# Two transformer blocks on one core: keeping the split weight blocks that two token streams share

## The chip, the cores and the metric

The kernel runs on one core of a Trainium2 chip. The metric is device time in microseconds (us) of one execution, as the median of several runs. Everything is float32 outside and inside; the large products are made in float32r, a form in which the tensor engine takes one pass per product, and float32's accuracy is kept by splitting each operand into a high and a low part and adding three products (high by high, high by low, low by high).

## The reference, cut to what matters

Two blocks follow each other on 512 tokens of 2048 channels. The first is a gated convolution beside a differential attention. The second has two recurrences (a gated delta rule of 8 heads and an RWKV-7 scan of 16 heads), and these run over a context of 256 tokens first and then over the 512 latent tokens. Both streams are multiplied by the same weight matrix:

```python
h = rmsnorm(x, norm_g[layer]) * (1.0 + scale[:, None]) + shift[:, None]
hc = rmsnorm(ctx, norm_g[layer]) * (1.0 + scale_c) + shift_c
u = h @ w_in[layer]
uc = hc @ w_in[layer]
ya_c, ya = gdn_mixer(uc[..., :GDN_COLS], u[..., :GDN_COLS], ...)
yb_c, yb = rwkv_mixer(uc[..., GDN_COLS:], u[..., GDN_COLS:], ...)
x = x + gate[:, None] * (jnp.concatenate([ya, yb], axis=-1) @ w_out[layer])
return rmsnorm(x, final_norm_g)
```

The context's own output isn't used; only the states that its recurrences leave go into the latent stream.

## The kernel before, in words

Activations lie with channels on partitions and tokens along the free dimension. The second block's input weights `w2` are 69 blocks of 128 output channels by 2048 input channels. `mblock` (L111) makes one block's product into a PSUM bank (pool `pd`, two banks) in two halves of 8 input tiles; `products` (L120) makes a half. It loads the half, 512 KB, into `wraw` (three buffers) by a DMA on SyncE's queue (L127), splits it (`split`, L103: a cast on ScalarE gives `whi`, L104, and a subtraction on VectorE gives `wlo`, L105), and issues 24 products (L136), three for each input tile. `whi` and `wlo` have two buffers each, so the split of one half waits until the tensor engine is done with the half before the last. While the context's gates, keys and values are made, every second subtraction goes to GpSimd (`K.on_pool = 2`).

The stages in the order of time, with the times of the profile:

- 0 to 456 us: the first block's modulation, gates and some steps of its convolution.
- 456 to 777 us: the context's products, 37 blocks or 74 halves with 256 columns each. These blocks are the gates (`B_GATE`), 8 keys and 8 values of the delta rule, 4 low-rank blocks (`B_LO`), and 8 keys and 8 values of the other recurrence. Their results go to DRAM as `kc` and `rc`. `ctx_gdn`, the delta rule over the context, runs in the gaps, head by head; a head loads `cgk` and `cgv` from `kc`.
- 777 to 2275 us: the rest of the first block with the remaining context recurrences in its gaps.
- 2275 to 3112 us: `mixers_gdn`. The gates and `B_LO` are first multiplied while `h` is made, in quarters of 4 input tiles (`K.pre` in `block1`); then for each of 8 heads the blocks Q, K, V, Z and `gdn_core`. The head's output goes out as `yd`. The last two heads also take the first pairs' inputs of the other recurrence (`mixed`: blocks R, K, V, Z).
- 3112 to 3900 us: `mixers_rwkv`, with the later pairs' `mixed` blocks and the first half of the output's products as filling.
- 3900 to 4056 us: the rest of the output's products and the final norm.

The program is written in Tile, which orders each engine's instructions ahead of time by priority and by its own estimate of when each is ready; matmuls of a burst of `K.burst` are put ahead of others (`FIRST`). Each engine, and SyncE's DMA queue, then works strictly in that order: a DMA whose wait isn't over holds up all behind it.

Of the kernel before, what the change touches and what calls it, by code (L numbers as in the profile page):

```python
# [55 lines left out]
EARLY, HELD = 6, 4     # gates made along with h, gates held back until the convolution's norm  # L56
# [8 lines left out]
def setup(ctx, tc, A):  # L65
# [14 lines left out]
    K.n_split = K.on_pool = 0  # L80
    K.cs, K.pre = {}, {}
# [29 lines left out]
def mblock(K, wap, act, T, k0=0, k1=16, half=8):  # L111
    """psum [128, T] = block^T . act, with act a list of (hi, lo) tiles for k = k0 .. k1."""
    ps = K.pd.tile([128, 512], F32, name="pd")
    for ka in range(k0, k1, half):
        products(K, ps, wap, act[ka - k0:], T, ka, min(half, k1 - ka), k0, k1)
        K.fill()
    return ps[:, :T]


def products(K, ps, wap, act, T, ka, w, k0, k1):  # L120
    """The w products from k = ka on of the block's in ps. K.burst of them follow each other, as the array is slow
    to change over from and to others."""
    nc, tc = K.nc, K.tc
    raw = K.wp.tile([128, 8, 128], F32, name="wraw")
    hi = K.wp.tile([128, 8, 128], F32R, name="whi", bufs=2)
    lo = K.wp.tile([128, 8, 128], F32R, name="wlo", bufs=2)
    nc.sync.dma_start(raw[:, :w], wap[:, ka:ka + w, :])  # L127
    K.n_split += 1
    split(K, hi[:, :w], lo[:, :w], raw[:, :w], nc.gpsimd if K.on_pool and K.n_split % K.on_pool == 0 else nc.vector)
    for k in range(w):  # L130
# [9 lines left out]
def rsqrt(K, pool, src, shape, a, eps, name, eng=None, exact=False):  # L140
    """(src * a + eps) ** -0.5, src may be in PSUM: a guess from the bits, then Newton's steps."""
# [21 lines left out]
def exp_acc(K, pool, x, shape, name):  # L163
    """exp to float32's accuracy: 2^n exactly, the rest from exp(r/2)^2 near 0."""
# [17 lines left out]
def silu2(K, pool, dst, src, name):  # L182
    """dst = 2 * silu(src)."""
    th = pool.tile(list(dst.shape), F32, name=name + "_th")
    K.nc.scalar.activation(th, src, AF.Tanh, scale=0.5)
    K.nc.vector.scalar_tensor_tensor(dst, th, 1.0, src, op0=ALU.add, op1=ALU.mult)


def ada_vec(K, pool, key, cols):
    """silu of the conditioning vectors, as the stationary columns of the modulation's products."""  # L190
# [10 lines left out]
def ada_steps(K, key, wname, bias, groups, nj, pe=True, pool=None):  # L201
    """In steps: K.mod[key][:, block, j] = silu(c_j) . w_ada + b_ada, channels on partitions; 512 columns a group.
    Without pe the vector engine sums over the 16 blocks of inputs, for j = 0."""
# [32 lines left out]
def colsum(K, src, T, w="ones", bank="px0"):  # L236
    """psum [128, T] = sum over partitions (of each half for bones), on every partition."""
# [5 lines left out]
def run(it, n=10000):  # L243
    """n more steps of it, if there are so many."""
# [4 lines left out]
class ChanSS:  # L249
    """Sums the squares of n channel tiles over all channels; rinv() gives (a * sum + eps) ** -0.5 on every  # L250
    partition. The tensor engine sums over the tiles, too, or else GpSimd does."""
# [29 lines left out]
def rsqrt_bcast(K, pool, p, row, T, a, eps, name, px, g):  # L281
    """psum [128, T] = (a * x + eps) ** -0.5 with x in psum p, tokens on partitions (g columns for each 128 of
    them); for g = 2 the columns go to a half of the partitions each. row [128, T] is overwritten."""
# [15 lines left out]
def load_rms(K, pool, src, T, name):  # L299
    """rsqrt(mean of squares over the channels + EPS) of a [16, 128, T] array in DRAM, on every partition."""  # L300
# [8 lines left out]
def modulate(*a):  # L309
    """hi/lo of xt * rinv * g * (1 + scale) + shift, xt = get(k), hi and lo in the tiles that put() returns."""  # L310
    return list(modulate_steps(*a))
# [24 lines left out]
# ------------------------------------------------------------------ unit lower triangular inverses  # L336
def inv64(K, pool, upool, nm, n, d, px, tmp):
    """nm [128, n, 64] holds -M^T of two 64 x 64 units a tile (halves of the partitions), M strictly
    lower in time order; tmp [128, n, 64] is overwritten. Returns U = ((I + M)^-1)^T alike, and T of the 32-blocks."""
# [38 lines left out]
    # 32 -> 64; e: the earlier 32-block of the unit, l: the later  # L378
# [29 lines left out]
# ------------------------------------------------------------------ gated delta rule  # L408
def gdn_gates(K, pool, kpool, ps, T, s):
    """ps [128, T]: rows 0-7 g d0, 32-39 g d1, 64-71 beta d0, 96-103 beta d1."""  # L410
# [23 lines left out]
    # cumulative sums over each 64 tokens: inside each 16, then of the 16s' totals  # L434
# [58 lines left out]
def cumsum(K, g):  # L493
    """In place over the last axis (64): pairs are summed first, then the sums' cumulative sums give the rest."""
# [13 lines left out]
def gdn_prep(K, pool, ps, T, ti, name, nb=2):  # L508
    """Centred convolution and silu of one channel tile, for q and k then unit columns a token; v is
    left doubled."""  # L510
# [26 lines left out]
def gdn_core(K, pool, cpool, h, q, k, v, T, s, gates, S):  # L537
    """One head of one stream. Returns the sum of both directions' outputs (channels on partitions) for
    the latent stream, else None; S[d] holds the states and is updated."""
# [5 lines left out]
    # row broadcasts of the cumulative gates, both directions at a time  # L545
# [26 lines left out]
    def gram(b, nm, mask):  # L572
        """b . k in compact form: [128, nt, 64] of each 64-chunk with itself, and with the tile's other."""
# [24 lines left out]
    for d in range(2):  # L598
# [31 lines left out]
        # dd: -M^T of the chunks; dx: -M^T from the first chunk to the second  # L630
        u64, u32, t32, ys = inv64(K, pool, pool, dd, nt, d, px[d], pool.tile([128, nt, 64], F32, name="iv_tmp"))
        # T of the first chunk: its 32-blocks and T_l Y between
# [29 lines left out]
        # the tail keys  # L662
# [1095 lines left out]
```

## Time and profile before

| what | value |
|---|---|
| time, median of 3 runs | 4048.28 us (4042.07 to 4054.17) |
| span of the profiled execution (it is none of the three; its own time isn't listed apart) | 4056.2 us |
| busy PE / DVE / ACT / POOL | 94% / 69% / 34% / 12% |
| moved by DMA | 497 MB, 123 GB/s over the span; 53 MB of it written to HBM |
| DMA of 512 KB halves of weights, median from issue to landing | 3.5 to 4.6 us |

PE is the tensor engine, DVE VectorE, ACT ScalarE, POOL GpSimd, SP SyncE with its DMA queue. Busy shares are averages over stages that have different limits, so the table says little about any one place; the stage windows further down are read for that. PE counts as busy from a matmul's start to its modelled end, and matmuls overlap, so a stage near 100% may still have matmuls that are further apart than they could be.

### The profile page before, as it was taken

The numbers are of one execution on the slowest core, as the hardware profiler recorded it, in microseconds if no ns is written. First come the engines' busy times: TensorE is split into PE (matmuls) and PEld (weight loads), VectorE is DVE, ScalarE is ACT, GpSimd is POOL, SyncE is SP. The second block draws the span as 40 slices with busy tenths as digits, with TensorE's granted clock in tenths as the row PEclk, the third lists the DMA queues.
The fourth block names the chain that finished last, engine by engine and source line by source line (L and its number), as shares of the span: only waits on it lengthen the run. The fifth ranks groups of instructions, "written<-read, shape, count | busy, mean of one in ns | idle before, by whom it ended". The sixth has DMA issues, their size and how long they took to land. (4 is left out here: it accounts for less than half of the span.)

```text
span 4056.2 us, 82730 instructions
## 1 busy us (share of the span) xinstructions
PE 3829.7 (94%) x33202; PEld 2916.8 (72%) x33202; DVE 2808.6 (69%) x7413; ACT 1389.2 (34%) x2825; POOL 479.8 (12%) x572
## 2 busy tenths in 40 slices
PE   8999878999999999999999799999999999999997
PEld 4676668876767767776887477877777777766776
DVE  3366787688777777744532977878667877777766
ACT  3312333323343434322322333333323443434333
POOL 0000221002110100000221301101001110111102
PEclk9999899999999999999999899999999998999998
DMA  8766435433334333424533332222223211222236
GB/s 320 266 212 200 157 127 165 146 113 110 126 114 125 104 104 99 149 91 143 207 113 122 104 96 69 71 72 74 81 84 107 67 64 55 76 67 88 91 120 203
DMA packets 213121, 497.01 MB, mean 123 GB/s; under 512 B 40576, under 2 KB 73600, under 8 KB 212736
## 3 DMA queue, kind: packets, MB, share of 16 engines
q1 hardware_dynamic: 212736, 491.72, 37.0%
q8 instruction: 261, 4.28, 0.4%
q14 instruction: 124, 1.02, 0.1%
HBM read 438.54 MB, written 53.08 MB: 121 GB/s over the span
## 5 line engine op out<-in xcount | busy, mean ns | idle before, releaser
L136 PE MATMUL pd<-big,whi 128*128 128x512 f32 x5344 | 1788.5, 412 | 9.1 <-ACT big L331 8.0
L136 PEld LDWEIGHTS pd<-big,whi 128*128 128x128 f32 x5344 | 965.7, 191 | 262.0 <-issue 27.8
L136 PE MATMUL pd<-big,wlo 128*128 128x512 f32 x2800 | 1114.0, 398 | 3.8 <-DVE wlo L105 3.8
L104 ACT CAST whi<-wraw 128x1024 fp32r<-128x1024 f32 (+2 forms) x500 | 506.7, 1014 | 1109.7 <-PE pd L136 1045.6
L105 DVE TENSOR_TENSOR wlo<-wraw,whi 128x1024 fp32r<-128x1024 f32 (+2 forms) x483 | 579.2, 1199 | 310.8 <-ACT whi L104 276.7
L136 PEld LDWEIGHTS pd<-big,wlo 128*128 128x128 f32 x2800 | 534.8, 191 | 128.0 <-DVE wlo L105 6.4
L136 PE MATMUL pd<-hc,whi 128*128 128x256 f32 x1184 | 236.3, 299 | 17.8 <-ACT gc_up L515 6.0
L136 PEld LDWEIGHTS pd<-hc,whi 128*128 128x128 f32 x1184 | 193.2, 200 | 23.4 <-ACT gc_up L515 6.4
L136 PE MATMUL pd<-hc,wlo 128*128 128x256 f32 x592 | 175.4, 297 | 28.3 <-DVE wlo L105 24.0
L136 PE MATMUL pd<-ext,whi 128*128 128x512 f32 x512 | 184.4, 401 | 3.8 <-DVE ext L105 3.8
L1075 DVE SCALAR_TENSOR_TENSOR cv_y<-cv_up,vec,cv_y 128x512 f32<-128x512 f32 x240 | 179.7, 749 | 4.7
L136 PE MATMUL pd<-fa,whi 128*128 128x512 f32 x448 | 153.1, 423 | 0.3 <-DVE wo L1462 0.2
L136 PEld LDWEIGHTS pd<-hc,wlo 128*128 128x128 f32 x592 | 117.9, 199 | 34.1 <-DVE wlo L105 27.8
L971 ACT ACTIVATE rg_zw<-rg_H,rg_wc 64x64 f32<-64x64 f32 x320 | 104.7, 343 | 47.1 <-DVE rg_H L989 38.7
L858 POOL TENSOR_TENSOR rg_bk<-rg_th,rg_L 64x512 f32<-64x512 f32 x48 | 67.7, 1410 | 425.5 <-ACT rg_L L837 193.0
L989 DVE SCALAR_TENSOR_TENSOR rg_H<-pc,rg_wc,rg_zw 64x64 f32<-64x64 f32 x320 | 90.5, 283 | 38.9 <-PE pc L981 30.5
L136 PEld LDWEIGHTS pd<-ext,whi 128*128 128x128 f32 x512 | 97.2, 190 | 27.8 <-DVE ext L105 4.6
L221 DVE SCALAR_TENSOR_TENSOR ada_ev<-wraw,cs_ada,ada_ev 128x512 f32<-128x512 f32 x120 | 94.8, 790 | 15.8 <-DMA wraw<-in_wada_dram 14.8
L520 DVE SCALAR_TENSOR_TENSOR gc_y<-gc_up,vec,gc_y 128x512 f32<-128x512 f32 (+1 forms) x160 | 103.2, 645 | 2.0
L136 PEld LDWEIGHTS pd<-fa,whi 128*128 128x128 f32 x448 | 82.2, 194 | 20.2 <-issue 1.1
L370 ACT COPY iv_y<-px 128x256 f32<-128x256 f32 (+2 forms) x112 | 33.0, 294 | 177.2 <-PE px L368 176.9
L906 PE MATMUL px<-rg_C,rg_bk 64*128 64x128 f32 x512 | 92.5, 311 | 0.3 <-DVE rg_C L909 0.3
(575 smaller groups left out, 5915.3 us busy)
## 6 DMA issues: line engine op xcount, KB each, us to landing
wraw<-in_w_dram SPq DMA_DIRECT2D x372, 512.0 KB, 3.6
wraw<-in_wada_dram SPq DMA_DIRECT2D x192, 512.0 KB, 4.6
wraw<-in_wo_dram SPq DMA_DIRECT2D x32, 512.0 KB, 3.5
sgl<-sgd SPq DMA_DIRECT2D x48, 256.0 KB, 3.4
wraw<-in_wout_dram SPq DMA_DIRECT2D x20, 512.0 KB, 4.1
wraw<-in_w_dram SPq DMA_DIRECT2D x32, 256.0 KB, 3.9
sgd<-msg SPq DMA_DIRECT2D x32, 256.0 KB, 3.7
wraw<-in_wco_dram SPq DMA_DIRECT2D x16, 512.0 KB, 3.5
```

The source lines that it names most:

```text
L104: K.nc.scalar.copy(hi, src)
L105: (eng or K.nc.vector).tensor_tensor(lo, src, hi.bitcast(F32), op=ALU.subtract)
L136: nc.tensor.matmul(ps[:, :T], lhsT=a[:, k], rhs=b, start=(n == 0), stop=(n == 3 * (k1 - k0) - 1))
L221: nc.vector.scalar_tensor_tensor(ev, raw[:, k], cs[:, kk, 0:1], ev, op0=ALU.mult, op1=ALU.add)
L370: nc.scalar.copy(ys, yp)
L520: nc.vector.scalar_tensor_tensor(y, up[:, t:t + T], w[:, t:t + 1], y, op0=ALU.mult, op1=ALU.add)
L858: nc.gpsimd.tensor_tensor(bk[uq, :, u], th[uq], F[uq], op=mul)
L906: nc.tensor.matmul(pg[:, m], lhsT=bk[q, 4 * r + m].rearrange("p x c -> p (x c)"), rhs=C[q, 4 * r + m, u], start=True, stop=True, tile_posi ...
L971: nc.scalar.activation(zw[hv[u], d], H[hv[u], ms[d], u], AF.Copy, scale=wn[hv[u], 4 * d + mn])
L989: nc.vector.scalar_tensor_tensor(Hn[hv[u], 4 * d + mn, u], pc3[hv[u], 2, d], wn[hv[u], 4 * d + mn], zw[hv[u], d], op0=mul, op1=ALU.add)
L1075: nc.vector.scalar_tensor_tensor(y, up[:, t:t + 512], w[:, t:t + 1], y, op0=ALU.mult, op1=ALU.add)
```

## The change

`products` no longer makes the two parts itself but asks `block_parts` for them. When the context's products are made (`keep`), each half's `whi` and `wlo` are also written to DRAM, 512 KB each. When a block with a key that was kept comes up for the latent stream, the two parts are loaded straight into `whi` and `wlo`, and there is no `wraw`, no cast and no subtraction. Blocks Q, Z, R and the second Z, which the context doesn't use, go the old way. Comments were dropped too, so line numbers differ: L127, L136, L104 and L105 of before are L132 (raw load), L153 (products) and `split`'s lines now; L129 loads a part and L138 stores one.

```diff
-def products(K, ps, wap, act, T, ka, w, k0, k1):
...
-    nc, tc = K.nc, K.tc
-    raw = K.wp.tile([128, 8, 128], F32, name="wraw")
+def block_parts(K, wap, ka, w, key, keep):
...
+    nc = K.nc
     hi = K.wp.tile([128, 8, 128], F32R, name="whi", bufs=2)
     lo = K.wp.tile([128, 8, 128], F32R, name="wlo", bufs=2)
+    if not keep and (key, 0) in K.parts:
+        for t, x in zip((hi, lo), K.parts[key, 8 * (ka // 8)]):
+            nc.sync.dma_start(t[:, :w].bitcast(F32), x[:, ka % 8:ka % 8 + w])
+        return hi, lo
+    raw = K.wp.tile([128, 8, 128], F32, name="wraw")
     nc.sync.dma_start(raw[:, :w], wap[:, ka:ka + w, :])
...
+    if keep:
+        K.parts[key, ka] = [K.dram.tile([128, 8, 128], F32, name=f"w{n}{key}_{ka}") for n in "hl"]
+        for t, x in zip((hi, lo), K.parts[key, ka]):
+            nc.sync.dma_start(x, t.bitcast(F32))
+    return hi, lo
+
+
+def products(K, ps, wap, act, T, ka, w, k0, k1, key=None, keep=False):
...
+    nc, tc = K.nc, K.tc
+    hi, lo = block_parts(K, wap, ka, w, key, keep)
...
-    return lambda b: mblock(K, K.A["w2"][b], hc, 256)
+    return lambda b: mblock(K, K.A["w2"][b], hc, 256, key=b, keep=True)
...
-                        products(K, ps, A["w2"][b], h[k:], 512, k, 4, 0, 16)
+                        products(K, ps, A["w2"][b], h[k:], 512, k, 4, 0, 16, b)
...
-        blk = lambda b: K.pre.pop(b) if b in K.pre else mblock(K, A["w2"][b], h, 512)
+        blk = lambda b: K.pre.pop(b) if b in K.pre else mblock(K, A["w2"][b], h, 512, key=b)
```

In the program as ordered, ACT has 78 casts fewer and DVE 78 subtractions fewer (70 of 1024 columns, 8 of 512); POOL has as many instructions as before. SP has 226 DMAs more: 148 stores, and two loads in place of one 78 times.

SP's queue while the context's keys and values are made (`wh_` and `wl_` are the parts in DRAM, with the first input tile of the half; `kc<-gk` is a finished key or value). Before:

```order
L1222 DMA kc<-gk 128x256
L127 DMA wraw<-in_w_dram 128x1024 x3
L1223 DMA kc<-gk 128x256
L127 DMA wraw<-in_w_dram 128x1024
L1222 DMA kc<-gk 128x256
```

With the change:

```order
L132 DMA wraw<-in_w_dram 128x1024 x3
L138 DMA wh_0<-whi 128x1024
L1240 DMA kc<-gk 128x256
L138 DMA wl_0<-wlo 128x1024
L1239 DMA kc<-gk 128x256
L138 DMA wh_8<-whi 128x1024
L138 DMA wl_8<-wlo 128x1024
L138 DMA wh_0<-whi 128x1024
L138 DMA wl_0<-wlo 128x1024
L132 DMA wraw<-in_w_dram 128x1024 x3
```

The raw loads now stand three at a time behind the six stores of the three halves before, the last of which waits for that half's subtraction.

PE around the last product of the context (`pd<-hc`). Before:

```order
L136 MATMUL pd<-hc,whi 128x256 x2
L136 MATMUL pd<-hc,wlo 128x256
L391 MATMUL px<-iv_t,gd_dd 32x32 x4
L686 MATMUL pc<-gd_vn,gd_ktl 128x128
L136 MATMUL pd<-big,whi 128x512 x2
```

With the change:

```order
L153 MATMUL pd<-hc,whi 128x256 x2
L153 MATMUL pd<-hc,wlo 128x256
L153 MATMUL pd<-big,whi 128x512 x2
L153 MATMUL pd<-big,wlo 128x512
...
L385 MATMUL px<-iv_t,gd_dd 32x32 x8
```

What stands ahead of this place has changed: of the 32 by 32 products `px<-iv_u,iv_y` of L374 (now L391), 32 for each head of `ctx_gdn`, 96 stood ahead of it and 192 do now. Three more heads of eight are ordered into the context's stage.

SP's queue at the seam of two heads of `mixers_gdn` (`gd_dd`, `gd_dx` and `gd_egt` are the head's gate rows, `yd<-gz` its finished output). Before:

```order
L553 DMA gd_dd<-gd_lat 64x4x64 x4
L556 DMA gd_dx<-gd_lat 64x4x64 x2
L127 DMA wraw<-in_w_dram 128x1024 x2
L547 DMA gd_egt<-gtd_lat 128x2x512
L127 DMA wraw<-in_w_dram 128x1024
L1445 DMA yd<-gz 128x512
L127 DMA wraw<-in_w_dram 128x1024 x5
```

With the change:

```order
L132 DMA wraw<-in_w_dram 128x1024 x2
L564 DMA gd_egt<-gtd_lat 128x2x512
L132 DMA wraw<-in_w_dram 128x1024
L1462 DMA yd<-gz 128x512
L129 DMA whi<-wh_0 128x1024
L129 DMA wlo<-wl_0 128x1024
L129 DMA whi<-wh_8 128x1024
L129 DMA wlo<-wl_8 128x1024
```

The parts of the next head's keys now come behind `yd<-gz`, each pair of loads into buffers that the tensor engine frees only two halves ahead of their use.

## Rows read from the trace of the kernel before

**Rows 1.** The page: busy us, share of the span and instructions of each engine.

```profile
PE 3829.7 (94%) x33202; PEld 2916.8 (72%) x33202; DVE 2808.6 (69%) x7413; ACT 1389.2 (34%) x2825; POOL 479.8 (12%) x572
```

**Rows 2.** Stage windows: PE, PEld, DVE, ACT, POOL busy, granted clock, DMA share, GB/s.

```profile
456.00:777.00 321.00, 273.37 (x2434) 253.24 (x2433) 260.26 (x708) 126.36 (x225) 65.41 (x89) 0.93 0.47 147
777.00:1700.00 923.00, 890.39 (x8362) 654.40 (x8357) 717.40 (x2097) 335.43 (x774) 95.52 (x118) 0.99 0.36 114
2275.00:2400.00 125.00, 117.20 (x548) 92.68 (x550) 100.82 (x201) 50.36 (x72) 19.32 (x28) 0.95 0.34 106
2400.00:3112.00 712.00, 699.48 (x6529) 555.11 (x6525) 533.31 (x1687) 226.56 (x442) 69.78 (x149) 0.99 0.25 79
3112.00:3900.00 788.00, 753.21 (x10060) 560.01 (x10061) 609.09 (x1780) 326.05 (x802) 101.28 (x87) 0.93 0.23 73
```

**Rows 3.** The same of the context's products alone (PE, PEld, DVE, ACT).

```profile
456.00:777.00 321.00, 251.70 (x1776) 230.59 (x1775) 9.63 (x16) 6.14 (x15) 0.93 0.47 147
```

**Rows 4.** Timeline of ACT: casts five in a row of the context's keys and values.

```profile
561.98 1.05 ACT L104 CAST whi<-wraw 128x1024 fp32r<-128x1024 f32 x1 [2.59 <-PE pd L136]
...
578.12 1.05 ACT L104 CAST whi<-wraw 128x1024 fp32r<-128x1024 f32 x1 [2.59 <-PE pd L136]
```

**Rows 5.** Tile whi, 456 to 777 us: ns min/median/max, first and last start.

```profile
L104 ACT CAST whi<-wraw x74: 1027/1047/1055, 463.6 to 776.8; 128x1024 fp32r<-128x1024 f32 x74
L105 DVE TENSOR_TENSOR wlo<-wraw,whi x57: 1182/1221/1359, 464.7 to 773.1; 128x1024 fp32r<-128x1024 f32 x57
L105 POOL TENSOR_TENSOR wlo<-wraw,whi x16: 2347/2439/4172, 473.0 to 607.6; 128x1024 fp32r<-128x1024 f32 x16
```

**Rows 6.** Timeline of PE: two products of one kind, 256 columns, three products apart.

```profile
604.73 0.40 PE L136 MATMUL pd<-hc,whi 128*128 128x256 f32 x2
...
605.09 0.40 PE L136 MATMUL pd<-hc,whi 128*128 128x256 f32 x2
```

**Rows 7.** DMA issues: KB each, median us from issue to landing.

```profile
wraw<-in_w_dram SPq DMA_DIRECT2D x372, 512.0 KB, 3.6
xd<-wo SPq DMA_DIRECT2D x32, 256.0 KB, 2.2
x1d<-out SPq DMA_DIRECT2D x16, 256.0 KB, 2.1
wraw<-in_w_dram SPq DMA_DIRECT2D x32, 256.0 KB, 3.9
```

**Rows 8.** Windows in the load-bound start, columns as in rows 2.

```profile
20.00:40.00 20.00, 17.49 (x85) 4.83 (x84) 7.43 (x12) 3.89 (x7) 1.27 (x1) 1.00 1.03 407
50.00:70.00 20.00, 19.27 (x113) 12.70 (x115) 3.12 (x6) 3.08 (x5) 0.00 (x0) 1.00 0.92 332
```

**Rows 9.** Waits of PE: 456 to 777 us the first, 2275 to 3112 us the second.

```profile
PE pd L136 <- DVE wlo L105: 24.0, 18, 3.6
...
PE pd L136 <- DVE wlo L105: 0.5, 1, 0.5
```

**Rows 10.** The chain that ended last: by engine; its start; first and last of 11 subtractions.

```profile
PE 17%; DVE 4%; DMA 1%; issue 1%; ACT 0%; POOL 0%; SPq 0%; DVEq 0%; ACTq 0%
...
3112.62 0.04 issue
...
3161.58 0.12 DVE wlo L105
...
3945.79 0.88 DVE wlo L105
```

**Rows 11.** Timeline of PE: 512 columns, three products apart, at a head's seam.

```profile
2566.43 0.62 PE L136 MATMUL pd<-big,whi 128*128 128x512 f32 x2
...
2567.11 0.62 PE L136 MATMUL pd<-big,whi 128*128 128x512 f32 x2
```

**Rows 12.** Waits of SP's queue, 2400 to 3100 us, for the store of yd.

```profile
SPq L1445 <- DVE iv_sh L351: 63.2, 6, 10.8
```

More of the change, by code (lines that the diff above doesn't have):

```diff
@@ L80, in setup @@
     K.n_split = K.on_pool = 0
+    K.parts = {}
     K.cs, K.pre = {}, {}
@@ L108, with mblock @@
 FIRST = 1000000
-def mblock(K, wap, act, T, k0=0, k1=16, half=8):
+def mblock(K, wap, act, T, k0=0, k1=16, half=8, key=None, keep=False):
     ps = K.pd.tile([128, 512], F32, name="pd")
     for ka in range(k0, k1, half):
-        products(K, ps, wap, act[ka - k0:], T, ka, min(half, k1 - ka), k0, k1)
+        products(K, ps, wap, act[ka - k0:], T, ka, min(half, k1 - ka), k0, k1, key, keep)
         K.fill()
     return ps[:, :T]
-def products(K, ps, wap, act, T, ka, w, k0, k1):
-    nc, tc = K.nc, K.tc
-    raw = K.wp.tile([128, 8, 128], F32, name="wraw")
+def block_parts(K, wap, ka, w, key, keep):
+    nc = K.nc
     hi = K.wp.tile([128, 8, 128], F32R, name="whi", bufs=2)
     lo = K.wp.tile([128, 8, 128], F32R, name="wlo", bufs=2)
+    if not keep and (key, 0) in K.parts:
[3 more added lines that the diff above has]
+    raw = K.wp.tile([128, 8, 128], F32, name="wraw")
     nc.sync.dma_start(raw[:, :w], wap[:, ka:ka + w, :])
```

## The prediction

> **What bounds the kernel now.** I read the page's busy shares first. The tensor engine is busy 94% of the span, VectorE 69%, ScalarE 34% [rows 1], so work taken from VectorE and ScalarE counts only where the tensor engine waits for it. The stage windows say where that is. In the latent delta rule (2400 to 3112 us) the tensor engine is busy 699.5 of 712 us, in the latent RWKV stage 753.2 of 788, in the short start of the latent stream 117.2 of 125, in the context's stage only 273.4 of 321 [rows 2]. The waits agree: over 2275 to 3112 us the tensor engine's largest wait for a subtraction `wlo` comes to 0.5 us, in the context's stage to 24.0 us in 18 waits [rows 9]. So the splits that the change removes lie where nearly nobody waits for them, and the stores that it adds lie where weights are already late.
>
> The context's stage is short of time per half, not of DMA: the DMA engines are busy 47% of it, at 147 GB/s [rows 2]. Four halves of keys and values take 578.12 - 561.98 = 16.1 us, 4.04 us a half [rows 4]; the tensor engine's own work in it is 24 products at a third of 605.09 - 604.73, 0.12 us, or 2.9 us [rows 6]. The rest is the cast (1.05 us), the subtraction (1.22 us on VectorE, 2.44 on GpSimd) [rows 5] and what else these engines have queued.
>
> The chain of waits covers the last stretch, from 3112.6 us on [rows 10]. The tensor engine has 17% of the span on it, VectorE 4%, ScalarE nothing that shows. Subtractions `wlo` are on it in 11 pieces of at most 1.2 us.
>
> **Term 1, the stores: +64 us.** Each of the context's 74 halves now moves three times 512 KB, 1.573 MB, in place of one. The load-bound start shows what the DMA engines give: 407 GB/s at best, 332 in another stretch at 92% [rows 8]. That is 3.9 to 4.7 us a half. The stage's other traffic (147 GB/s over 321 us less 74 x 0.524 MB, 8 MB) adds 0.3 us. So 4.2 to 5.0 us a half is the DMA's own pace, and 4.6 its middle, against 4.04 us now.
>
> SP's order adds a loop of waits: three raw loads, then the six stores of these halves, then the next three loads. Without any queueing I count from the issue of the loads: the first lands at 3.6 us [rows 7], its cast ends at 4.65 and its subtraction at 5.9 [rows 5]; its products run to about 8.5; its low part's store lands at 5.9 + 2.8 = 8.7 (256 KB lands in 2.1 to 2.2 us [rows 7], and another 256 KB at 407 GB/s takes 0.65). Only then may the third half's split overwrite the buffer: cast 8.5 to 9.6, subtraction to 10.8, and behind its store the next loads go out. That is 10.8 us for three halves, 3.6 us each. This loop alone would fit into today's pace. But it needs the DMA engines at once, which three halves keep busy 12.6 to 15 us, and while the third half is cast nothing new is queued for them: one cast per turn, 0.3 us a half. I take 4.6 + 0.3 = 4.9 us, so (4.9 - 4.04) x 74 = +64 us. The lower end is the DMA at its best rate, 4.2 us and +12; the upper end is the poor rate plus the fixed part of one load's landing (3.6 less 1.29 us of transfer) exposed once per turn, 5.0 + 0.8 = 5.8 us and +130. I stay near the middle, since both rates in rows 8 are measured.
>
> The Trainium skill, "DMA: Bandwidth & Descriptors", section Bandwidth, says that between HBM and SBUF the HBM's share of a core, about 358 GB/s, binds. The 407 GB/s of this trace [rows 8] disagree for a single core; by the rule a half would take 4.4 + 0.6 us, and the time would come out some 7 us higher. The same page, section Anatomy of one DMA, puts most of a fixed 2 us down to the write's receipt, heaviest for HBM. Here stores into DRAM land sooner (2.1 us) than loads of the same 256 KB (3.9) [rows 7]; by its fit a 512 KB store would take 3.2 us, an estimate that adds 0.4 us a turn, about 10 us.
>
> **Term 2, heads that move: -16 us.** Three more heads of the context's delta rule are ordered into the longer stage, where the tensor engine has gaps, and leave the stage behind it, where it is busy 890 of 923 us [rows 2]. In the stage now, all tensor work besides the context's products is 273.4 - 251.7 = 21.7 us [rows 2, 3], for three heads, the norms and the gates. I take three quarters, 16 us; between 0 (if VectorE, with three heads' work more on its 260 us, can't follow) and 22.
>
> **Term 3, latent splits gone: -11 us.** 70 casts of 1.05 us, 70 subtractions of 1.22 and 8 of half the size go, about 78 us of ScalarE and 90 of VectorE. In the delta rule's stage I cost their absence at nothing: the tensor engine's products cover them, and if they did not, its whole idle time there is 12.5 us [rows 2]. In the RWKV stage 12 of the shared blocks, 24 halves, lift 24 x 1.22 = 29 us off VectorE's 609, or 5%; VectorE has 4% of 4056 us, 162 us, on the chain [rows 2, 10], and 5% of it is 8 us. In the start of the latent stream the tensor engine is idle 7.8 us [rows 2]; 3 of it for splits is my guess. Bounds: 0, and half of all idle time in the three windows (7.8 + 12.5 + 34.8), 28 us.
>
> **Term 4, parts that come late: +6 us.** A latent half's parts can be loaded only once the half before the last has left the buffers. In dense stretches a half lasts 24 x 0.227 = 5.4 us (2567.11 - 2566.43 for three products [rows 11]); the high part lands at about 3.6 us and the low one 1.3 to 1.6 us later, 5.2 at most. So it just fits, where nothing stands ahead on SP's queue. At the delta rule's head seams the store of `yd` does, for which SP waited 63.2 us over six heads [rows 12]; `rl`, `lr` and `yr` stand so in the RWKV stage. Before, three raw buffers gave these waits room; now a wait there holds the next parts. I take one exposed us at six of the 14 seams, 6 us; at most a landing of 3 us at each, about 40. Less than nothing it can't be.
>
> Sum: 64 - 16 - 11 + 6 = **+43 us**. The profiled execution's span is 4056.2 us, 8 us above the median of the runs, and its own time isn't given, so I lay the sum on the median: 4048.3 + 43 = **4091 us**.
>
> **Rivals.**
> - The latent stream gains more than the context loses. The place is the RWKV stage and the start of the latent stream, where VectorE's queue decides. For it: VectorE is busy 77% of the RWKV stage and the granted clock there is 0.93, since the tensor engine has gaps; fewer subtractions close them. Against it: `wlo` is a small part of the chain. Price: -28 (half of all idle), -16, and a context stage at the best DMA rate, +12: 4016 us. It decides as soon as a context half takes less than about 4.5 us. Chance 0.16.
> - The context's loss is given back almost whole: 4.45 us a half (+30), -16, -11: 4051 us. For it: 407 GB/s was reached. Chance 0.17.
> - The parts come late throughout: term 4 at its upper end, 4091 + 34 = 4125 us. For it: one queue that is waited on in order, two buffers. Against it: a latent half lasts over 9 us on average, 712 us for some 79 halves. Chance 0.12.
> - The clock falls in the context's stage. It is 0.93 there already [rows 2]; at the lower level of 1.2 GHz a half's products take 5.8 us, more than 4.9. A third of the halves so would add 25 x 0.9, 22 us: 4113 us. I count it within the forecast's range.
>
> That the splits would not vanish is excluded: the ordered program lacks all 78.
>
> **How the numbers follow.** Forecast 0.55, the rivals 0.16, 0.17 and 0.12. About 0.3%, 12 us, is what a measurement of this kernel can tell from no change. The second rival and the lower edge of the forecast make the middle: faster 0.16, same 0.18, slower 0.66. The range takes in the poor end of term 1 beside the others' values (+117) and, below, most of the first rival: 4025 to 4165 us.
>
> **What would show it.** Context stage: about 385 us in place of 321 with the DMA share near 90% and 300 GB/s or more, casts 4.9 us apart, waits of ScalarE for stores. Delta rule's stage: still 705 to 720 us. RWKV stage: a few us shorter. I am wrong if the context's stage stays below 335 us, if the tensor engine idles over 20 us for DMA `whi` or `wlo` in the latent stages, or if these shrink by more than 30 us.

## The result and the profile after

The changed kernel takes 4227.39 us, median of 4 runs (4218.73 to 4229.73); the kernel before took 4045.18 us beside it (4 runs, 4036.64 to 4054.17). The ratio is 1.0447, with a 95% interval of 1.0426 to 1.0467. The forecast was 4091 us and its range ended at 4165.

The page of the changed kernel, first busy time and share of the span by engine, answering to [rows 1], then the DMA issues with KB and median us to landing:

```profile
PE 3884.7 (92%) x33202; PEld 2965.0 (70%) x33202; DVE 2740.7 (65%) x7335; ACT 1317.6 (31%) x2747; POOL 475.4 (11%) x572
...
wh<-whi SPq DMA_DIRECT2D x74, 512.0 KB, 3.6
wl<-wlo SPq DMA_DIRECT2D x74, 512.0 KB, 3.7
whi<-wh SPq DMA_DIRECT2D x70, 512.0 KB, 3.5
wlo<-wl SPq DMA_DIRECT2D x70, 512.0 KB, 4.3
```

VectorE and ScalarE lost 68 us and 72 us of work, where the forecast counted about 90 and 78. TensorE does the same 33202 matmuls and is busy 55 us longer. Where the time went, the products of the context say. The next lines are those of the tile `hc`, which give the first and the last start (`456.6 to 776.6`); first the kernel before, then the changed one:

```profile
L136 PE MATMUL pd<-hc,wlo x592: 274/281/582, 456.6 to 776.6; 128*128 128x256 f32 x198
```

```profile
L153 PE MATMUL pd<-hc,wlo x592: 274/282/583, 455.8 to 979.3; 128*128 128x256 f32 x198
```

From the first product of any kind to the last (455.7 to 776.6, and 454.9 to 979.3) the stage grew from 321 to 524 us, by 203. Behind it three more landmarks give the rest. They are the first load of the latent stream's rows (`ext`, 2215.8 and 2365.4 us), the last store of `yd`, which ends the delta rule's stage (3060.8 and 3206.0), and the end (4056.2 and 4217.0). The changed kernel's lag is 150, 145 and 161 us there. So 53 of the 203 us are given back before the latent stream starts; the start and the delta rule gain 4 more; the last stretch loses 16.

The windows of the changed kernel (PE, PEld, DVE, ACT, POOL busy, granted clock, DMA share, GB/s): the context's stage, then from the latent stream's start to the last `yd`, then the rest:

```profile
455.00:980.00 525.00, 377.61 (x3165) 333.74 (x3166) 339.33 (x1118) 151.78 (x303) 74.51 (x124) 0.79 0.68 241
...
2365.00:3206.00 841.00, 790.96 (x6829) 617.38 (x6828) 582.10 (x1771) 213.46 (x431) 97.67 (x179) 0.98 0.34 116
3206.00:4217.00 1011.00, 938.38 (x11454) 706.91 (x11453) 726.25 (x2068) 379.06 (x928) 138.59 (x129) 0.93 0.32 105
```

Against [rows 2] the reader is to see three things in the first line. The DMA engines are busy 68% of the stage at 241 GB/s: they aren't the limit that the forecast made them. TensorE idles 147 us (it was 48). And the granted clock fell from 0.93 to 0.79, which is a share of the stage at the lower of its two levels (1.2 GHz in place of 2.4).

### The profile page after: what moved, and what is told of

It reads as the page before. It is cut to its first block, busy times and chain, and to the rows that moved or that the text cites. A ratio compares the mean times of both kernels' runs of the same rounds, so it can differ in the third digit from the quotient of the medians.

```text
span 4217.0 us, 82887 instructions
## 1 busy us (share of the span) xinstructions
PE 3884.7 (92%) x33202; PEld 2965.0 (70%) x33202; DVE 2740.7 (65%) x7335; ACT 1317.6 (31%) x2747; POOL 475.4 (11%) x572
## 5 line engine op out<-in xcount | busy, mean ns | idle before, releaser
L153 PE MATMUL pd<-big,whi 128*128 128x512 f32 x5344 | 1782.9, 411 | 8.1 <-ACT big L348 8.0
L153 PEld LDWEIGHTS pd<-big,whi 128*128 128x128 f32 x5344 | 969.4, 191 | 263.8 <-issue 28.4
L153 PE MATMUL pd<-big,wlo 128*128 128x512 f32 x2800 | 1113.2, 398 | 2.0 <-DMA wlo<-wl 1.7
L105 ACT CAST whi<-wraw 128x1024 fp32r<-128x1024 f32 (+2 forms) x422 | 428.3, 1015 | 1028.4 <-PE pd L153 908.5
L106 DVE TENSOR_TENSOR wlo<-wraw,whi 128x1024 fp32r<-128x1024 f32 (+2 forms) x405 | 487.1, 1203 | 353.2 <-ACT whi L105 313.0
L153 PEld LDWEIGHTS pd<-big,wlo 128*128 128x128 f32 x2800 | 535.0, 191 | 124.6 <-DMA wlo<-wl 2.5
L153 PE MATMUL pd<-hc,whi 128*128 128x256 f32 x1184 | 278.8, 335 | 50.4 <-ACT whi L105 44.1
L153 PEld LDWEIGHTS pd<-hc,whi 128*128 128x128 f32 x1184 | 227.2, 234 | 61.1 <-ACT whi L105 48.6
L153 PE MATMUL pd<-hc,wlo 128*128 128x256 f32 x592 | 194.4, 329 | 33.8 <-DVE wlo L106 24.7
L153 PE MATMUL pd<-ext,whi 128*128 128x512 f32 x512 | 184.3, 400 | 3.8 <-DVE ext L106 3.8
L153 PEld LDWEIGHTS pd<-hc,wlo 128*128 128x128 f32 x592 | 137.5, 232 | 40.1 <-DVE wlo L106 28.6
L153 PE MATMUL pd<-fa,whi 128*128 128x512 f32 x448 | 151.0, 418 | 0.3 <-DVE wo L1479 0.2
L153 PEld LDWEIGHTS pd<-ext,whi 128*128 128x128 f32 x512 | 97.3, 190 | 27.5 <-DVE ext L106 4.3
L393 DVE COPY_PREDICATED iv_u<-cpi,px 128x256 f32<-128x256 int32 (+2 forms) x112 | 38.0, 339 | 93.4 <-PE px L391 81.7
```

The lines of the kernel that those rows point to most:

```text
L105: K.nc.scalar.copy(hi, src)
L106: (eng or K.nc.vector).tensor_tensor(lo, src, hi.bitcast(F32), op=ALU.subtract)
L153: nc.tensor.matmul(ps[:, :T], lhsT=a[:, k], rhs=b, start=(n == 0), stop=(n == 3 * (k1 - k0) - 1))
L393: nc.vector.copy_predicated(u32, K.cp[d, lev].unsqueeze(1).to_broadcast([128, n, 32]), zp)
```

## The experiments

Stage is the time from the first to the last start of the context's products in the profiled execution, "last stretch" the time from the last store of `yd` to the end of its span.

| run | median, us | ratio to before, 95% interval | stage, us | last stretch, us |
|---|---|---|---|---|
| before | 4045 to 4056 | | 321 | 995 |
| changed | 4227 | 1.0447 (1.0426 to 1.0467) | 524 | 1011 |
| loads alone | 4082 | 1.0066 (1.0042 to 1.0091) | 320 | 1025 |
| stores alone | 4203 | 1.0365 (1.0334 to 1.0397) | 525 | 986 |
| stores of an eighth of the bytes | 4083 | 1.0075 (1.0047 to 1.0103) | 325 | 1020 |
| stores from GpSimd's queue | 4144 | 1.0230 (1.0190 to 1.0270) | 382 | 1016 |
| raw loads from ScalarE's queue | 4143 | 1.0224 (1.0200 to 1.0248) | 383 | 1008 |
| raw loads first, one queue | 4210 | 1.0375 (1.0343 to 1.0408) | 504 | 1003 |
| three queues | 4140 | 1.0227 (1.0211 to 1.0243) | 388 | 1004 |
| half the bytes, GpSimd's queue | 4094 | 1.0114 (1.0086 to 1.0142) | 352 | 1006 |
| half the bytes, raw loads from ScalarE's | 4097 | 1.0119 (1.0096 to 1.0143) | 343 | 1023 |
| three heads in the stage | 4235 | 1.0446 (1.0416 to 1.0475) | 472 | 1009 |
| no heads in the stage | 4239 | 1.0465 (1.0426 to 1.0503) | 431 | 1004 |
| before, no heads in the stage | 4052 | 0.9995 (0.9979 to 1.0012) | 282 | 984 |
| loads alone, delta rule only | 4054 | 1.0003 (0.9982 to 1.0023) | 322 | 990 |
| loads alone, GpSimd's queue | 4066 | 1.0035 (1.0016 to 1.0055) | 320 | 997 |
| loads alone, more buffers | 4058 | 1.0023 (1.0010 to 1.0037) | 322 | 986 |
| before, latent raw loads from GpSimd | 4090 | 1.0097 (1.0075 to 1.0120) | 320 | 1018 |

### Loads alone, stores alone

Only the gate's block is stored, and all latent blocks load its parts:

```diff
-    if keep:
+    if keep and key == B_GATE:
         K.parts[key, ka] = [K.dram.tile([128, 8, 128], F32, name=f"w{n}{key}_{ka}") for n in "hl"]
...
+    elif keep:
+        K.parts[key, ka] = K.parts[B_GATE, ka]
```

> The loads of the latent stream alone: only the gate's block is stored, and all 37 latent blocks load those two parts (same bytes and queue as in the changed kernel, wrong weights). Theory A (the cost is all in the context's stage, the latent stream gains a little): the stage of the context's products is as long as before, 321 us, and the whole takes 4015 to 4045 us. Theory B (the loads cost time in the RWKV stage, which was 16 us longer after the change): stage as before, but last yd to end longer than before by 10 us or more, whole 4045 to 4070 us.

The stage is as long as before, and the kernel is slower all the same, with the last stretch longer by 29 us. Theory B holds in its place and sign: the latent stream loses by the change. The loss is larger than its range (4045 to 4070 us).

The other half alone: the latent stream goes the raw way.

```diff
-    if not keep and (key, 0) in K.parts:
+    if False:
```

> The stores alone: the latent stream takes its weights the old way, by raw load and split. If stores and loads cost independently (the loads some 25 us, by the run with loads alone), the stage stays near 524 us and the whole takes 4180 to 4210 us. If the latent parts gain something beside the stores after all (prediction's terms 3 and 4), 4215 us or more.

4203 us: the stores cost what the changed kernel loses less the loads' 25. The two parts of the change add up, and nothing in the latent stream pays for the stores.

### Bytes or queue

An eighth of each store, with as many stores on the same queue:

```diff
         for t, x in zip((hi, lo), K.parts[key, ka]):
-            nc.sync.dma_start(x, t.bitcast(F32))
+            n = 8 if key == B_GATE else 1
+            nc.sync.dma_start(x[:, :n], t[:, :n].bitcast(F32))
+        if key != B_GATE:
+            K.parts[key, ka] = K.parts[B_GATE, ka]
```

> The changed kernel with every store cut to an eighth of its bytes (one of eight 128-column pieces; the gate's block in full, and the latent loads read that block's parts, so the weights are wrong). The number of stores, their place in SP's queue and what each waits for stay. Theory 1 (the prediction's: bytes, DMA's pace): the context's products take at most 345 us of the changed kernel's 524, whole at most 4060 us. Theory 2 (SP's queue in order: raw loads stand behind stores that wait for their cast and subtraction): the stage stays at 460 us or more, whole 4150 us or more.

The stage is back at 325 us; the whole, at 4083, is above theory 1's 4060, as the latent loads and their loss were kept. That looked like theory 1, but the run isn't clean: in the order that Tile made of it, one raw load also follows nearly every half's two stores, where the changed kernel has three raw loads and then six stores, and only three heads of the delta rule stand in the stage, not six. So the next two runs keep all bytes and move one side to another queue. First the stores to GpSimd's:

```diff
-            nc.sync.dma_start(x, t.bitcast(F32))
+            nc.gpsimd.dma_start(x, t.bitcast(F32))
```

> All stores of the changed kernel issued from GpSimd's queue in place of SP's, same bytes. Theory 2 (SP's queue): raw loads are no longer behind the stores, stage 350 to 410 us, whole 4060 to 4130 us, though GpSimd's own subtractions now stand behind stores that wait. Theory 1 (bytes): stage within 30 us of 524, whole 4200 us or more. Theory 3 (buffers of the parts held by stores until they land): also unchanged, with casts waiting for stores.

Then the raw loads to ScalarE's, with the stores left on SP's:

```diff
-    nc.sync.dma_start(raw[:, :w], wap[:, ka:ka + w, :])
+    (nc.scalar if keep else nc.sync).dma_start(raw[:, :w], wap[:, ka:ka + w, :])
```

> The context's raw loads issued from ScalarE's queue, the stores stay on SP's. Theory 2: the raw loads wait for no store, stage 350 to 420 us, whole 4060 to 4140 us. Theory 1 and theory 3: stage within 30 us of 524, whole 4200 us or more.

Both give the same: half the loss is gone. The stages lie in theory 2's ranges, the whole times 14 and 3 us above them. The windows of the two stages, columns as above:

```profile
458.60:840.80 382.20, 300.02 (x2452) 276.88 (x2452) 257.25 (x711) 128.45 (x228) 135.60 (x235) 0.87 0.89 318
```

```profile
456.50:839.50 383.00, 302.80 (x2490) 275.51 (x2490) 269.41 (x765) 130.12 (x235) 65.16 (x95) 0.89 0.87 316
```

Here the stage is what the forecast described: 382 us (it said about 385), a DMA share near 90%, over 300 GB/s. So some 61 us go with the stores wherever they are issued, and the rest of the 203 with the one queue. A third arrangement asked whether the 61 are still a queue's waits: raw loads on ScalarE's queue, `whi` stored from SP's, `wlo` and the latent loads on GpSimd's.

```diff
-    nc.sync.dma_start(raw[:, :w], wap[:, ka:ka + w, :])
+    (nc.scalar if keep else nc.sync).dma_start(raw[:, :w], wap[:, ka:ka + w, :])
...
-        for t, x in zip((hi, lo), K.parts[key, ka]):
-            nc.sync.dma_start(x, t.bitcast(F32))
+        for t, x, q in zip((hi, lo), K.parts[key, ka], (nc.sync, nc.gpsimd)):
+            q.dma_start(x, t.bitcast(F32))
```

> All bytes of the changed kernel on three queues: the context's raw loads from ScalarE's, the cast parts stored from SP's, the subtracted parts from GpSimd's, and the latent loads from GpSimd's. Bytes as the limit: the stage stays at 370 to 390 us, DMA share 0.87 or more, and the whole takes 4115 to 4140 us. Rival (what is left of the stores' cost is still waiting in a queue): stage 345 to 365 us, whole 4090 to 4115 us. Both: slower than before still.

388 us at a DMA share of 0.89: the rival falls. Three ways to issue the same bytes end within 7 us of each other.

Is it the order on the one queue? The raw loads get the earliest priority, and one or two of them then stand between the stores of each half:

```diff
+    K.tc.cur_priority -= FIRST * keep
     nc.sync.dma_start(raw[:, :w], wap[:, ka:ka + w, :])
+    K.tc.cur_priority += FIRST * keep
```

> The changed kernel, all stores and loads on SP's queue and all bytes as they were, but the context's raw loads are given the scheduler's earliest priority, so that one raw load or two stand between the stores of each half, where the changed kernel has three raw loads and then the six stores of three halves. Theory 2 as it now stands (of the stage's 203 us some 60 are the stores' bytes and the rest is that a turn's raw loads stand behind all stores of the turn before): stage 375 to 420 us, whole 4130 to 4165 us, as with another queue. Rival (one queue for both is what costs, however ordered): stage 480 us or more, whole 4190 us or more.

A miss for theory 2 as it stood: 504 us, with six heads in the stage as in the changed kernel. The waits of ScalarE and of SP's queue in that stage (total us, times, longest) show what took the place:

```profile
ACT whi L105 <- DMA wh<-whi: 78.6, 30, 7.8
```

```profile
SPq L133 <- DVE wlo L106: 80.4, 25, 8.7
```

Now the raw loads, which wait for VectorE to free a raw buffer, hold the stores behind them (80.4 us), and the casts wait for those stores to release `whi` (78.6 us). So it isn't this order or that: on one queue that works in order, either the loads wait behind stores that want their split, or the stores behind loads that want their buffer.

### The heads that moved

The kernels with raw loads and full stores on SP's queue also have some 730 more TensorE instructions in the stage (x3165 against x2434 in [rows 2]), the three heads of term 2; those with another queue have not (x2452, x2490). Queue and heads had to be told apart. In these runs SP's order of raw loads and stores stays that of the changed kernel, but for the last few:

```diff
...
-                ctx_gdn(K, pool)
+                ctx_gdn(K, pool, range(3))
                 ctx_dense_rwkv(K, blk, cl)
+                ctx_gdn(K, pool, range(3, 8))
```

> The changed kernel with three heads of the context's delta rule ordered before the RWKV blocks' products and five behind them, so that the stage holds three as before the change and not six; SP's order of raw loads and stores is that of the changed kernel. Theory 2 (SP's queue makes the excess over the 61 us of bytes): stage 470 us or more, and what the moved heads gave back behind the stage is lost, whole 4225 to 4290 us. Theory 4 (the moved heads make it: their work stands ahead of the splits on VectorE and TensorE): stage 380 to 420 us, whole 4130 to 4175 us.

The window of its stage, columns as above:

```profile
455.00:928.00 473.00, 334.30 (x2474) 302.12 (x2474) 268.96 (x725) 130.64 (x230) 65.91 (x95) 0.79 0.71 258
```

With all eight heads behind the products, in the changed kernel and, as a control, in the kernel before:

```diff
-                ctx_gdn(K, pool)
                 ctx_dense_rwkv(K, blk, cl)
+                ctx_gdn(K, pool)
```

> The changed kernel with all eight heads ordered behind the RWKV blocks' products: no head's work in the stage, SP's order as in the changed kernel. Theory 2: stage 440 us or more, whole 4250 us or more. Theory 4: stage 360 to 400 us; the whole then 4140 to 4190 us, since three heads more run behind the stage than before.

> The control for the run without heads: the kernel before with all eight heads behind the RWKV blocks' products. If heads in the stage cost as much there as they give back behind it: whole within 10 us of 4050 and the stage some 15 to 25 us shorter. If they were hidden in gaps: stage within 10 us of 321, whole 4065 to 4085 us. If the stage's loss to them is larger than their gain, this beats both kernels: 4020 to 4040 us.

Heads are neutral within the intervals of these ratios. Six, three and none in the changed kernel's stage make it 524, 472 and 431 us, and the whole 1.0447, 1.0446 and 1.0465: what they cost in the stage comes back behind it. The control does the same (39 us shorter, more than the 15 to 25 expected; ratio 0.9995). Theory 4 falls. Theory 2 holds with three heads; without heads its stage and its whole are 9 and 11 us below the bounds it named (440 and 4250). With equal heads the change costs the stage 472 - 321 = 151 us with three and 431 - 282 = 149 with none. With three heads, 61 of these are left on another queue; the other 90 are the one queue's. Without heads no run used another queue, so the division isn't measured there.

### One turn of the loop

The run without heads shows the loop of three halves undisturbed. SP's queue from one batch of raw loads to the next (start, duration, line):

```profile
755.71 0.42 SPq L138 DMA_DIRECT2D wl<-wlo  x1
756.19 1.78 SPq L132 DMA_DIRECT2D wraw<-in_w_dram  x3
762.61 0.33 SPq L138 DMA_DIRECT2D wh<-whi  x1
763.87 0.33 SPq L138 DMA_DIRECT2D wl<-wlo  x1
764.29 0.41 SPq L138 DMA_DIRECT2D wh<-whi  x1
765.22 0.48 SPq L138 DMA_DIRECT2D wl<-wlo  x1
769.86 0.32 SPq L138 DMA_DIRECT2D wh<-whi  x1
771.51 0.32 SPq L1256 DMA_DIRECT2D rc<-rm  x1
771.88 0.42 SPq L138 DMA_DIRECT2D wl<-wlo  x1
772.36 0.44 SPq L132 DMA_DIRECT2D wraw<-in_w_dram  x1
```

ScalarE's casts in it, with the idle time before each and what ended it:

```profile
761.54 1.04 ACT L105 CAST whi<-wraw 128x1024 fp32r<-128x1024 f32 x1 [7.39 <-DMA wraw<-in_w_dram]
762.89 1.05 ACT L105 CAST whi<-wraw 128x1024 fp32r<-128x1024 f32 x1 [0.30 <-DMA wraw<-in_w_dram]
768.79 1.04 ACT L105 CAST whi<-wraw 128x1024 fp32r<-128x1024 f32 x1 [4.85 <-PE pd L153]
```

And TensorE, its first product of the turn and two of one kind later, three products apart, then the window of the turn:

```profile
762.64 0.50 PE L153 MATMUL pd<-hc,whi 128*128 128x256 f32 x2 [4.80 <-ACT whi L105]
...
764.92 0.63 PE L153 MATMUL pd<-hc,whi 128*128 128x256 f32 x2
...
765.56 0.63 PE L153 MATMUL pd<-hc,whi 128*128 128x256 f32 x2
```

```profile
756.20:772.40 16.20, 10.64 (x65) 10.23 (x65) 4.13 (x5) 3.51 (x4) 0.00 (x0) 0.79 0.80 301
```

The turn takes 772.36 - 756.19 = 16.2 us where the forecast counted 10.8. Three places make the 5.4 us:

- The first cast starts 5.35 us after the issue, not 3.6: the loads go out right behind the last store of the turn before (755.71) and share the DMA engines with it. 1.75 us.
- TensorE, after 4.80 us without work, does three products in 765.56 - 764.92 = 0.64 us, where [rows 6] has 0.36. That is the lower clock (granted 0.50 from 764.0 to 769.3 us), and a half's products take some 5 us where 2.9 were counted. The third cast waits for them: it starts 7.25 us after the first, counted 4.9. 2.35 us.
- The last store stands behind `rc<-rm`, a result of the half before, and the next loads go out 0.5 us after it: 3.6 us after the third cast's start, counted 2.3. 1.3 us.

Meanwhile no raw load is on its way while the third half is split. For scale, an estimate: at the 316 GB/s of the runs with another queue, the nine transfers of a turn (9 x 0.524 MB) take 14.9 us. A loop of 10.8 us would have hidden behind that, one of 16.2 does not. The turn shown is shorter than the average: 431 us for 74 halves are 17.5 us for three, and 472 us, with three heads, are 19.1. What lengthens those wasn't taken apart.

### Half the bytes

Only the cast parts are stored, from GpSimd's queue, and then from SP's with the raw loads on ScalarE's. The first of the two:

```diff
-        K.parts[key, ka] = [K.dram.tile([128, 8, 128], F32, name=f"w{n}{key}_{ka}") for n in "hl"]
-        for t, x in zip((hi, lo), K.parts[key, ka]):
-            nc.sync.dma_start(x, t.bitcast(F32))
+        x = K.dram.tile([128, 8, 128], F32, name=f"wh{key}_{ka}")
+        nc.gpsimd.dma_start(x, hi.bitcast(F32))
+        K.parts[key, ka] = [x, x]
```

> As the run with all stores on GpSimd's queue, but only the cast part is stored (half the bytes and half the stores; the latent stream loads it in both places, so the weights are wrong). Bytes as the limit: loads of 47 MB (147 GB/s over before's 322 us) and 39 MB of stores at the 317 GB/s of the full stores need 271 us, less than the stage had, so the stage takes 322 to 345 us and the whole 4075 to 4100 us. Rival (each store's wait and landing cost, not the bytes): half of the 61 us or more stay, stage 350 us or more, whole 4105 us or more.

> Half the stores and bytes again (the cast parts alone, loaded in both places by the latent stream), but the stores stay on SP's queue and the raw loads go to ScalarE's, so that no store stands behind GpSimd's subtractions. If those held the stores in the run of half the bytes on GpSimd's queue: stage 322 to 338 us, whole 4070 to 4090 us. If the cost of the stores goes with their bytes, also below DMA's limit, because a part's buffer is held until its store has landed: stage 342 to 360 us, whole 4090 to 4115 us.

352 and 343 us: neither a limit by bytes (it left nothing to pay) nor quite a share by stores. The first run's stage falls in the rival's range and its whole in the other one; the second run's figures fall in its second range. In the first, ScalarE's largest wait is for stores to land and release `whi`:

```profile
ACT whi L105 <- DMA wh<-whi: 46.1, 16, 8.0
```

In the second this wait isn't among ScalarE's seven largest, and 22 us stay. A full set costs 61, a half 22 to 31, an eighth (as many stores as the full set) 4: the cost goes about with the bytes, also at a DMA share of 0.72. Which wait carries the 22 us wasn't settled. More buffers for the parts weren't tried in this stage, because SBUF has less than 4 KB of a partition left there.

### The latent loads

Which loads cost? The edits of this section are against the run with loads alone. First only those of the delta rule:

```diff
-    elif keep:
+    elif keep and key < B_RR:
         K.parts[key, ka] = K.parts[B_GATE, ka]
```

> The loads alone as in the first run, but only for the gate's, key and value blocks of the delta rule (17 of 37); the RWKV blocks are split as before. If the loss of the run with all loads (4082 against 4056 us) sits in the RWKV stage's loads, this takes 4045 to 4062 us and the stretch from the last yd to the end is within 6 us of before's 995. If it is spread or a matter of the order alone, 4065 to 4085 us.

Neutral (1.0003): the loss is the RWKV stage's. Then all part loads from GpSimd's queue (`nc.gpsimd` for `nc.sync` in the part load), and on SP's queue with more buffers:

> The loads alone as in the first run, but issued from GpSimd's queue. Theory C (on SP's queue the part loads wait for TensorE to free their two buffers, 151 us in the RWKV stage, and hold the other transfers behind them): the loss of 25 us goes, whole 4045 to 4065 us, unless GpSimd's own work is held instead. Theory D (the stage is TensorE's, and another order of its work and a lower clock make the loss): still 4070 to 4095 us.

```diff
     if not keep and (key, 0) in K.parts:
+        if ka % 16 >= 8:
+            hi, lo = (K.wp.tile([128, 8, 128], F32, name="wraw").bitcast(F32R) for _ in "hl")
```

> The loads alone as in the first run, all on SP's queue, but the second half of each block lands in the idle raw buffers, so that the part loads have more buffers and wait less for TensorE on SP's queue. Theory C (what waits behind the part loads on SP's queue makes the loss): whole 4050 to 4068 us and the RWKV stretch within 10 us of before's 995. Theory D (order and clock of TensorE's work): 4070 to 4095 us.

By the medians GpSimd's queue takes about half of the loss away (1.0035, whose interval still meets that of loads alone; 4066 us is just outside theory C's range), more buffers two thirds (1.0023). The last stretch of loads alone and of the run with more buffers, columns as above:

```profile
3056.00:4081.00 1025.00, 953.41 (x11455) 717.19 (x11454) 726.61 (x2070) 379.88 (x928) 138.94 (x129) 0.92 0.31 103
```

```profile
3070.00:4056.00 986.00, 920.02 (x11455) 695.18 (x11453) 721.37 (x2070) 379.66 (x928) 140.66 (x129) 0.95 0.32 107
```

The same TensorE work takes 33 us less busy time, at a higher clock. Theory C's wait, SP's queue waiting for TensorE to free a part's buffer, fell less (RWKV stage, loads alone, then more buffers):

```profile
SPq L129 <- PE pd L155: 151.3, 22, 14.1
```

```profile
SPq L131 <- PE pd L157: 132.8, 17, 25.0
```

And the kernel before waits longer than either there, with its raw loads, for VectorE:

```profile
SPq L127 <- DVE wlo L105: 186.3, 22, 19.6
```

Over all that weight loads wait for in that stage, SP's queue waits 315 us before, 352 with loads alone and 336 with more buffers, while the last stretches are 995, 1025 and 986. So theory C gave the place and the times, but its waits don't follow the loss, and what lowers the clock with part loads stays open.

Would the kernel before profit from another queue for its latent weights?

```diff
-    nc.sync.dma_start(raw[:, :w], wap[:, ka:ka + w, :])
+    (nc.gpsimd if T == 512 else nc.sync).dma_start(raw[:, :w], wap[:, ka:ka + w, :])
```

> Not the change but the kernel before, with the latent stream's raw weight loads (512 columns) issued from GpSimd's queue in place of SP's, since the part loads did better there than on SP's. If what stands behind a weight load on SP's queue costs the kernel before something too (its raw loads wait 186 us there for VectorE's subtraction in the RWKV stage): 4020 to 4043 us, faster than both. If three raw buffers are cover enough: 4043 to 4056 us, no difference. If GpSimd's own work is held up by loads that wait: 4056 to 4090 us.

No: 1.0097, and 4090 us is in the third range. GpSimd does wait long before it issues loads, with all that it has to compute behind them:

```profile
POOL wraw L127 <- DVE wlo L105: 1249.7, 239, 24.7
```

But the other engines hardly wait more for GpSimd than before: over the whole run TensorE 20 us against 18, VectorE 5 against 3, ScalarE 79 against 94. So that GpSimd's held work makes the loss isn't shown, and its cause stays open.

No version found beats the kernel before.

## Why the prediction was wrong, step by step

**Term 1 failed, in its loop of waits.** The sentence "this loop alone would fit into today's pace" is the step: 10.8 us a turn were counted, 16.2 measured in the turn shown and 17.5 on average. It was counted with each step at its time of before: the first load's landing without the stores ahead of it, the products at the full clock, and no other store in the queue. Because the loop was set below the DMA's pace, DMA's pace was taken as the limit, and with one queue it isn't (share 0.68). What was left out is the 90 us of the queue. The price of the bytes came out near, +64 forecast and +61 to +68 on other queues, but in part by luck. The forecast set 4.9 us a half against 4.04, a pace read from four halves; the whole stage ran at 321 / 74 = 4.34 us a half before and at 382 / 74 = 5.16 on GpSimd's queue, so both were some 0.3 us too low. Nor do the runs show that DMA's pace alone makes those 61 us: half the bytes still cost 22 to 31 at a DMA share of 0.72, and with the stores on GpSimd's queue TensorE is busy 300 us with nearly the work that took 273, at a granted clock of 0.87. The fourth rival named the falling clock, put a third of the halves at the lower level and priced it at 22 us; it is a part of the loop, not a case beside it.

On what the engines give, the Trainium skill ("DMA: Bandwidth & Descriptors", section Bandwidth) sets a core's share of HBM at about 358 GB/s, each, where both cores of a pair stream. The mixed traffic of the stage with another queue reached 316 and 318, below it, so these runs don't show that limit; the loads of [rows 8] reached 407. By the fit in its section Anatomy of one DMA, which the page gives for DMAs that GpSimd issues, a 512 KB store would take 3.2 us, an estimate. Here stores took 3.6 and 3.7 us from SP's queue, and 6.7 and 7.0 when GpSimd issued them, at a DMA share of 0.89; the measurement decides. On queues the same page (section SWDGE vs HWDGE vs iDMA, "Issuing engines are not separate DMA queues") says that issuing from several engines saves only the sequencer's time, usually small. Here it saved 90 us of the stage at equal heads (472 to 382) and 2.2% of the whole (1.0447 to 1.0230), because the issuing queue waits in its order; the measurement decides.

**Term 2, heads that move: no room in the stage.** Forecast -16 as if their work found room there. The three heads cost it 524 - 472 = 52 us, and against the kernel before 53 come back behind it: -1 in the sum. Against the changed kernel with three heads the trace would give more: that one lags 162 us at the first load of the latent stream (2378.3 less 2215.8), the one with six 150, which makes the heads -13 and the stores' part +162. The ratios, 1.0447 and 1.0446, show no gain, but their intervals are too wide to exclude it. So a gain isn't refuted, but the free room is: the bound of 22 us counted TensorE's time for three heads alone, and not the waits of a head's chain. The lower bound, 0, did name VectorE; its work in the stage rose from 260 to 339 us.

**Term 3, splits gone, and term 4, parts late.** The start and the delta rule gained 4 us, and loads there are neutral, as forecast (nothing and 3). The RWKV stage was to be 8 us shorter; the last stretch, which holds it, lost 16, and by loads alone 29. In the runs with all its weights raw on SP's queue this stretch takes 984 to 995 us, in those with part loads from that queue into two buffers 1003 to 1025. With more buffers it is 10 us shorter than before, near term 3's size, but within the spread of raw loads. Terms 3 and 4 together were thus too favourable: term 4 priced one late landing at six seams, and what the part loads cost beyond that, at a lower clock of TensorE, has no shown cause. TensorE waits for late parts itself only little: 2 us between 2430 and 4060 us, so that my sign for this rival, over 20 us of TensorE's idle for the parts, wouldn't have shown it.

Forecast against measured, in us: stores +64 and +151; heads -16 and -1; splits gone and parts late together -5 and +11 in this trace (-4.4 and +15.6; loads alone +25). The sums are +43 and +161, the latter between the two spans. A slip in the prediction's range changes nothing: the poor end of term 1 beside the others' values is 130 - 16 - 11 + 6 = +109, not +117.

## What to carry to other kernels

Before putting stores on the queue that prefetches, ask what each waits for: a store of a made value waits for the engines, and on a queue that works in order all prefetching waits with it. Count such a loop with the times that hold inside it (landing beside the stores, products at the lower clock after each gap, every other transfer in the queue), since it is these that decide whether the loop or the bytes is the limit. And work removed from engines that nobody waits for bought nothing here, while the loads that replaced it, alone, cost 25 us in the stretch that TensorE bounds.

## What the runs showed of the hardware

- TensorE's clock turns a small gap into a larger one: after 4.80 us without work three products took 0.64 us in place of 0.36, at a granted clock of 0.50, and with raw loads and stores on the one queue the whole stage had 0.79, with six, three and no heads in it.
- Loads and stores together kept the DMA engines busy 87 to 89% of stages of 382 to 388 us, at 314 to 318 GB/s.
- Three ways of issuing the same bytes (SP and GpSimd, SP and ScalarE, all three) gave stages of 382 to 388 us; one queue for both gave 472 with as many heads in it.
